# A hybrid encoder step on one core: value projection with one shared tile for the blocks' last 32 tokens, and the sampled tokens' output product with high and low parts as one operand of 64 columns

## The chip, the cores and the metric

The kernel runs on one core of a Trainium2 chip. The metric is the device time of one execution in microseconds (us), as the median of several runs. The engines are PE (matrix multiply, with PEld for the loads of its stationary operand), DVE (vector), ACT (scalar), POOL (GpSimd) and SP, which only issues transfers. Each engine works through its own queue in the order of the program that was built for it; semaphores tie the queues together. A matmul has a stationary operand of up to 128 columns and a moving operand of up to 512 columns, and adds into a bank of PSUM.

## The reference, cut to what matters

Two inputs go through the same two layers: a prompt of 2048 tokens and 32 sampled tokens that continue earlier states, 2080 tokens of width 1024 in all.

```python
# layer A: gated delta rule, then an output product and a layer norm
out = o.reshape(b, l, A_VW).astype(x.dtype) @ w_out
return layer_norm(DN_ALPHA * x + out, ln_g, ln_b), new_buf, s_new
# between the layers: one shared K and V
kv = h @ w_kv
k = rope_partial(kv[..., :B_KVW].reshape(b, l, B_KV_HEADS, B_HD), pos)
v = kv[..., B_KVW:].reshape(b, l, B_KV_HEADS, B_HD)
# layer B: sliding-window attention, then an output product and a layer norm
out = (o * jax.nn.silu(z)) @ w_out
return layer_norm(DN_ALPHA * x + out, ln_g, ln_b)
```

V has 4 heads of 64, so 256 columns. The output products are 1024 x 1024 per token.

## The kernel before, in words

All large products are in fp32 precision built from a rounded type: each operand x is split into a high part (x rounded) and a low part (x minus the high part), and a product is the sum of three matmuls, high x high, high x low and low x high. With 1024 = 8 x 128 rows to contract, a product of one tile takes 8 x 3 = 24 matmuls.

The program runs in stages. First come layer A's projections, then the delta rule over chunks of 128 tokens with the sampled tokens as a first, short chunk. Beside and behind it runs layer A's output product (class O1 with OutNorm, tile by tile of 128 tokens; the 17th and last tile holds the 32 sampled tokens). Each tile there: OutNorm.split makes the parts `ghi` and `glo` (L1091 on ACT, L1092 on DVE) while the tile before is multiplied; OutNorm.tile multiplies for two halves of 512 columns (L1105 to L1107), scales the residual and adds the product (L1110), takes statistics (L1111, L1113), forms the inverse root by Newton steps and normalizes (L1127, L1129); the rows are stored (L1186), turned by PE transposes (L1156), copied (L1158) and stored again as columns (L1160). In this stage the order on PE and DVE is that of the code.

Class P2 then reads those columns back as five blocks of 416 tokens: P2.load brings a block in four pieces over the queues of SP and ACT (L1228) into two staging buffers, and `split_acts` makes its parts (L68 on ACT, L69 on DVE for blocks 2 to 4). Blocks 0 and 1 are loaded early. P2 computes gate products (gate: L1313 to L1316, with the matmuls of `project`, L77 to L79), then the values (P2.values), then the rotated K and Q projections (P2.rotated), then more gates. From here on a scheduler sets the order on every engine by simulated times, so that instructions of a later stage may stand ahead of those of an earlier one where their buffers are free.

P2.values, at L1263 to L1276: for each block it goes through the 416 tokens in tiles of 128, 128, 128 and 32. A tile is 24 matmuls with the tokens as stationary columns and 256 value columns as the moving operand (L1272 to L1274), a copy from PSUM on ACT (L1275) and a store on SP (L1276) to the scratch `bv`. The values' weights are split at L1261 and L1262.

P2.rotated interleaves its ten slabs of weights (L46, L53, L54; five blocks each) with `keep_out_weights` (L992 to L999): layer B's output weights are read in 16 steps into one of two buffers of the pool `wo` (tag `wo_parts`), split on ACT (L995) and POOL (L996), and stored on SP (L994, L999) to the scratch `wob`, from which layer B's output stage reads them. The rotation (L1246 to L1250) uses ACT, DVE and POOL; its results are stored on SP.

Layer B's attention works on chunks of 64 queries; Attention.finish does the output product of a tile of 128 tokens: it loads the residual rows `r` (L1396, two buffers), splits (L1399 on ACT, L1400 on POOL), multiplies (L1411 to L1413), scales and adds (L1414, L1415), and normalizes either through ACT and POOL (L1424 to L1426) or, for the very last tile, on DVE (L1430, L1432), and stores `y` (L1434). The sampled tokens' tile is finished last but one, and the last tile is that of tokens 768 to 895 (the chunks run from 14 to 31 and then from 0 to 13); both take their two halves from a tile of two PSUM banks that the scores used before.

Of the kernel before, what the change touches and what calls it, by code (L numbers as in the profile page):

```python
# [10 lines left out]
F32 = mybir.dt.float32  # L11
F32R = mybir.dt.float32r
I32 = mybir.dt.int32
AF = mybir.ActivationFunctionType
ALU = mybir.AluOpType
# [4 lines left out]
D = 1024  # L20
NP = 2048
NS = 32
NT = NP + NS
TB = 416
NB = NT // TB
KC = D // 128
H = 8
ALPHA = 4.0 ** 0.25
# [67 lines left out]
class P1:  # L96
# [166 lines left out]
    def split(self):  # L263
        if self.fetched is not None:
            self.next = split_fetched(self.nc, self.wp, self.fetched, self.sub)
            self.fetched = None
# [794 lines left out]
    return gt, bt  # L1061


class OutNorm:


# [20 lines left out]
    def split(self, g, n):  # L1087
        nc = self.nc
        ghi = self.two.tile([128, KC, 128], F32R, tag="g_hi", name="g_hi")
        glo = self.two.tile([128, KC, 128], F32R, tag="g_lo", name="g_lo")  # L1090
        nc.scalar.copy(ghi[:, :, :n], g[:, :, :n])  # L1091
        nc.vector.tensor_tensor(out=glo[:, :, :n], in0=g[:, :, :n], in1=ghi[:, :, :n], op=ALU.subtract)  # L1092
        return ghi, glo

    def tile(self, parts, r, n, tail=False):

        nc, V = self.nc, self.nc.vector
        ghi, glo = parts
        st = self.two.tile([128, 2, 6], F32, tag="st", name="st")
        w = self.w  # L1100
        for c in range(2):
            cs = slice(c * 512, c * 512 + 512)
            ps = self.pp.tile([128, 512], F32, tag="po", name="po")
            for k in range(KC):
                nc.tensor.matmul(ps[:n], ghi[:, k, :n], w[0][:, k, cs], start=(k == 0), stop=False)  # L1105
                nc.tensor.matmul(ps[:n], ghi[:, k, :n], w[1][:, k, cs], start=False, stop=False)  # L1106
                nc.tensor.matmul(ps[:n], glo[:, k, :n], w[0][:, k, cs], start=False, stop=(k == KC - 1))  # L1107
                if k % 2 == 1:
                    yield 6 * 0.227
            V.scalar_tensor_tensor(out=r[:n, cs], in0=r[:n, cs], scalar=ALPHA, in1=ps[:n], op0=ALU.mult, op1=ALU.add)  # L1110
            V.bn_stats(out=st[:n, c, :], in_=r[:n, cs])  # L1111
        mv = self.two.tile([128, 2], F32, tag="mv", name="mv")
        V.bn_aggr(out=mv[:n], in_=st[:n])  # L1113
        ve = self.two.tile([128, 1], F32, tag="ve", name="ve")
        V.tensor_scalar(out=ve[:n], in0=mv[:n, 1:2], scalar1=LN_EPS, scalar2=None, op0=ALU.add)
        rs = rsqrt_newton(nc, self.two, ve, n, 1, "ln")
        tabs = self.tabs
        if not tail:
            nb = self.two.tile([128, 1], F32, tag="nb", name="nb")
            V.scalar_tensor_tensor(out=nb[:n], in0=mv[:n, 0:1], scalar=-1.0, in1=rs[:n], op0=ALU.mult, op1=ALU.mult)  # L1120
            nc.scalar.activation(r[:n], r[:n], AF.Identity, bias=nb[:n, 0:1], scale=rs[:n, 0:1])
            nc.gpsimd.tensor_tensor(out=r[:n], in0=r[:n], in1=tabs[0][:n], op=ALU.mult)
            nc.gpsimd.tensor_tensor(out=r[:n], in0=r[:n], in1=tabs[1][:n], op=ALU.add)
        else:
            for c in range(2):
                cs = slice(c * 512, c * 512 + 512)
                V.scalar_tensor_tensor(out=r[:n, cs], in0=r[:n, cs], scalar=mv[:n, 0:1], in1=tabs[0][:n, cs],  # L1127
                                       op0=ALU.subtract, op1=ALU.mult)
                V.scalar_tensor_tensor(out=r[:n, cs], in0=r[:n, cs], scalar=rs[:n, 0:1], in1=tabs[1][:n, cs],  # L1129
                                       op0=ALU.mult, op1=ALU.add)  # L1130
        yield r
# [63 lines left out]
class P2:  # L1195
# [57 lines left out]
    def values(self):  # L1253
        nc = self.nc
        vh = self.resl.tile([128, KC, 256], F32R, tag="cos", name="vh")
        vl = self.resl.tile([128, KC, 256], F32R, tag="sin", name="vl")
        for i in range(2):
            ks = slice(i * 4, i * 4 + 4)
            vr = self.wp.tile([128, 4, 256], F32, tag="w_raw", name="vr", bufs=1)
            nc.scalar.dma_start(vr[:], self.I["w_v"][:, ks, :])  # L1260
            nc.scalar.copy(vh[:, ks], vr[:])  # L1261
            nc.gpsimd.tensor_tensor(out=vl[:, ks], in0=vr[:], in1=vh[:, ks], op=ALU.subtract)  # L1262
        for b in range(NB):  # L1263
            xh, xl = self.x[b]
            for m0 in range(0, TB, 128):
                m = min(128, TB - m0)
                ms = slice(m0, m0 + m)
                a = self.wk.tile([128, 256], F32, tag="ra", name="va")
                ps = self.ps()
                po = ps[:m, 0:256]  # L1270
                for k in range(KC):
                    nc.tensor.matmul(po, xh[:, k, ms], vh[:, k, :], start=(k == 0), stop=False)  # L1272
                    nc.tensor.matmul(po, xl[:, k, ms], vh[:, k, :], start=False, stop=False)
                    nc.tensor.matmul(po, xh[:, k, ms], vl[:, k, :], start=False, stop=(k == KC - 1))  # L1274
                nc.scalar.copy(a[:m, :], po)  # L1275
                nc.sync.dma_start(self.T["bv"][b * TB + m0:b * TB + m0 + m, :], a[:m, :])  # L1276

    def rotated(self):
        nc, I, O, T = self.nc, self.I, self.O, self.T
# [39 lines left out]
class Attention:  # L1319
# [73 lines left out]
    def finish(self, t0, n, graw, late=False, tail=False):  # L1393
        nc, V, pool = self.nc, self.nc.vector, self.otwo
        r = pool.tile([128, D], F32, tag="r", name="r")
        nc.sync.dma_start(r[:n], self.T["h"][t0:t0 + n, :])  # L1396
        ghi = pool.tile([128, KC, 128], F32R, tag="g_hi", name="g_hi")
        glo = pool.tile([128, KC, 128], F32R, tag="g_lo", name="g_lo")
        nc.scalar.copy(ghi[:, :, :n], graw[:, :, :n])  # L1399
        nc.gpsimd.tensor_tensor(out=glo[:, :, :n], in0=graw[:, :, :n], in1=ghi[:, :, :n], op=ALU.subtract)  # L1400
        st = pool.tile([128, 2, 6], F32, tag="st", name="st")
        w, tabs = self.w, self.tabs
        both = self.scores_tile() if late else None
        for c in range(2):
            cs = slice(c * 512, c * 512 + 512)
            if late:
                ps = both[:, c].rearrange("p u k -> p (u k)")
            else:
                ps = self.pp.tile([128, 512], F32, tag="po", name="po")[:]
            for k in range(KC):  # L1410
                nc.tensor.matmul(ps[:n], ghi[:, k, :n], w[0][:, k, cs], start=(k == 0), stop=False)  # L1411
                nc.tensor.matmul(ps[:n], ghi[:, k, :n], w[1][:, k, cs], start=False, stop=False)  # L1412
                nc.tensor.matmul(ps[:n], glo[:, k, :n], w[0][:, k, cs], start=False, stop=(k == KC - 1))  # L1413
            V.scalar_tensor_tensor(out=r[:n, cs], in0=r[:n, cs], scalar=ALPHA, in1=ps[:n], op0=ALU.mult, op1=ALU.add)  # L1414
            V.bn_stats(out=st[:n, c, :], in_=r[:n, cs])  # L1415
        mv = pool.tile([128, 2], F32, tag="mv", name="mv")
        V.bn_aggr(out=mv[:n], in_=st[:n])
        ve = pool.tile([128, 1], F32, tag="ve", name="ve")
        V.tensor_scalar(out=ve[:n], in0=mv[:n, 1:2], scalar1=LN_EPS, scalar2=None, op0=ALU.add)
        rs = rsqrt_newton(nc, pool, ve, n, 1, "ln")  # L1420
        if not tail:
            nb = pool.tile([128, 1], F32, tag="nb", name="nb")
            V.scalar_tensor_tensor(out=nb[:n], in0=mv[:n, 0:1], scalar=-1.0, in1=rs[:n], op0=ALU.mult, op1=ALU.mult)
            nc.scalar.activation(r[:n], r[:n], AF.Identity, bias=nb[:n, 0:1], scale=rs[:n, 0:1])  # L1424
            nc.gpsimd.tensor_tensor(out=r[:n], in0=r[:n], in1=tabs[0][:n], op=ALU.mult)
            nc.gpsimd.tensor_tensor(out=r[:n], in0=r[:n], in1=tabs[1][:n], op=ALU.add)  # L1426
        else:
            for c in range(2):
                cs = slice(c * 512, c * 512 + 512)
                V.scalar_tensor_tensor(out=r[:n, cs], in0=r[:n, cs], scalar=mv[:n, 0:1], in1=tabs[0][:n, cs],  # L1430
                                       op0=ALU.subtract, op1=ALU.mult)
                V.scalar_tensor_tensor(out=r[:n, cs], in0=r[:n, cs], scalar=rs[:n, 0:1], in1=tabs[1][:n, cs],  # L1432
                                       op0=ALU.mult, op1=ALU.add)
        nc.sync.dma_start(self.O["y"][t0:t0 + n, :], r[:n])  # L1434
# [374 lines left out]
```

## Time and profile before

| what | us |
|---|---|
| median of three runs | 2256.95 |
| lowest and highest of them | 2256.91, 2264.41 |
| the profiled execution | 2253.47 |
| its span in the trace | 2251.5 |

The profile is of one execution. Its page gives busy times of each engine as a share of the span, the chain of work that ended last (followed back from the end through whatever released each step), and groups of instructions by line. In a row of a group, "x16 | 6.4, 396 | 0.8" means 16 instructions, 6.4 us busy, 396 ns each by the trace, and 0.8 us in which the engine sat idle just before them. A matmul's recorded duration holds its way through the array, so that neighbours overlap: the pace of matmuls is read from the distance between their starts. In the rows of the timeline, the first number is the start in us from the start of the span, the second the duration, and square brackets give an idle time before it with what ended it. In stretches of the span, each engine's busy time stands with its number of instructions, followed by the granted clock of PE as a share of full speed, the share of time in which the transfer engines were busy, and their rate.

### The profile page before, as it was taken

How to read it: one execution, taken by the hardware profiler on the slowest of the kernel's cores; microseconds unless marked ns; L12 is line 12 of the kernel's file. 1: busy time of each engine (PE TensorE's matmuls, PEld its weight loads, DVE VectorE, ACT ScalarE, POOL GpSimd, SP SyncE). 2: the span in 40 equal slices, each digit the busy share in tenths (PEclk: the TensorE clock that was granted, in tenths of full speed). 3: DMA queues.
4: the chain of work that ended last, by engine and by line, in shares of the span. 5: the costliest groups of instructions: out<-in, count | busy, mean ns of one | idle time of the engine just before them, and what ended most of it. 6: DMA issues, size and time to landing. Idle time of an engine off the chain costs nothing.

```text
span 2251.5 us, 36813 instructions
## 1 busy us (share of the span) xinstructions
PE 2180.5 (97%) x13810; PEld 1996.7 (89%) x13810; DVE 1372.5 (61%) x2709; ACT 897.3 (40%) x2230; POOL 836.6 (37%) x1185
## 2 busy tenths in 40 slices
PE   8999999999999999999899999999999999999997
PEld 6999999999999888898888887999999987778884
DVE  3666566743486677778868874124442235668774
ACT  4444444433223666667641212311112235445541
POOL 1422121212111577767721201324442124556563
PEclk9999999999999999999999999999999999999999
DMA  5222222323534243335526765732122277233311
GB/s 193 67 70 74 72 71 69 109 92 117 143 106 152 95 136 121 121 127 202 188 96 209 227 189 166 244 131 75 66 73 73 83 177 251 75 94 96 111 61 52
DMA packets 250530, 274.49 MB, mean 122 GB/s; under 512 B 76096, under 2 KB 195200, under 8 KB 250080
## 3 DMA queue, kind: packets, MB, share of 16 engines
q1 hardware_dynamic: 238352, 248.84, 35.2%
q10 hardware_dynamic: 12000, 23.30, 2.9%
q8 instruction: 109, 1.79, 0.3%
q14 instruction: 69, 0.57, 0.1%
HBM read 168.53 MB, written 103.92 MB: 121 GB/s over the span
## 4 chain that ended last, share of the span: by engine, by line
PE 84%; ACT 7%; DVE 4%; DMA 2%; POOL 2%; issue 1%; ACTq 0%; SPq 0%; DVEq 0%; POOLq 0%
PE ps L77 16%; PE ps L79 16%; PE ps L78 16%; PE ot L1526 4%; PE po L1105 3%; PE po L1107 3%; PE po L1106 3%; PE po L1411 2%; PE po L1413 2%; PE po L1412 2%; PE S L1505 2%; PE tr L1520 2%; PE vp L714 1%; ACT kd L588 1%; PE op L732 1%
## 5 line engine op out<-in xcount | busy, mean ns | idle before, releaser
L77 PE MATMUL ps<-act_hi,w_hi 128*128 128x416 f32 x2000 | 707.0, 354 | 8.2 <-ACT act_hi L68 4.5
L79 PE MATMUL ps<-act_hi,w_lo 128*128 128x416 f32 x2000 | 705.1, 353 | 1.8 <-POOL w_lo L54 1.2
L78 PE MATMUL ps<-act_lo,w_hi 128*128 128x416 f32 x2000 | 701.9, 351 | 0.1
L77 PEld LDWEIGHTS ps<-act_hi,w_hi 128*128 128x128 f32 x2000 | 377.0, 189 | 13.6 <-ACT act_hi L68 5.2
L79 PEld LDWEIGHTS ps<-act_hi,w_lo 128*128 128x128 f32 x2000 | 376.1, 188 | 6.7 <-POOL w_lo L54 1.7
L78 PEld LDWEIGHTS ps<-act_lo,w_hi 128*128 128x128 f32 x2000 | 376.4, 188 | 5.1 <-DVE act_lo L69 0.8
L54 POOL TENSOR_TENSOR w_lo<-w_raw,w_hi 128x1024 fp32r<-128x1024 f32 x51 | 135.3, 2652 | 547.9 <-ACT w_hi L53 490.8
L196 DVE SCALAR_TENSOR_TENSOR y<-R,convw,y 128x2083 f32<-128x2083 f32 x72 | 173.7, 2414 | 109.7 <-ACT y L194 74.2
L572 POOL TENSOR_TENSOR tm<-L,Tt 128x60 f32<-128x60 f32 (+19 forms) x373 | 139.7, 375 | 123.7 <-DVE tm L572 51.7
L1513 POOL TENSOR_TENSOR P<-P,sm 128x384 f32<-128x384 f32 (+2 forms) x128 | 100.5, 807 | 180.0 <-DVE sm L1390 102.4
L575 POOL TENSOR_TENSOR Tt<-Tt,tm 128x60 f32<-128x60 f32 (+19 forms) x373 | 152.9, 410 | 29.2
L1386 ACT ACTIVATE P<-S,nm 128x192 f32<-128x192 f32 (+2 forms) x260 | 104.6, 418 | 93.7 <-DVE nm L1379 40.7
L227 ACT COPY R<-ps 128x416 f32<-128x416 f32 (+1 forms) x144 | 61.2, 448 | 199.2 <-PE ps L79 174.4
L53 ACT CAST w_hi<-w_raw 128x1024 fp32r<-128x1024 f32 x62 | 65.0, 1048 | 137.4 <-PE ps L78 111.8
L1248 POOL TENSOR_TENSOR rs<-rs,sin 128x416 f32<-128x416 f32 x50 | 71.2, 1424 | 116.3 <-DVE rs L1247 102.0
L1105 PE MATMUL po<-wo_hi,g_hi 128*128 128x512 f32 (+1 forms) x272 | 110.2, 405 | 1.8 <-DVE r L1110 1.1
L1107 PE MATMUL po<-wo_hi,g_lo 128*128 128x512 f32 (+1 forms) x272 | 106.9, 393 | 0.0
L1106 PE MATMUL po<-wo_lo,g_hi 128*128 128x512 f32 (+1 forms) x272 | 106.6, 392 | 0.0
L1526 PE MATMUL ot<-pt,vd 128*128 128x256 f32 x372 | 98.7, 392 | 1.6 <-ACT pt L1522 1.2
L1411 PE MATMUL po<-wo,g_hi 128*128 128x512 f32 x240 | 99.4, 414 | 0.0
L1413 PE MATMUL po<-wo,g_lo 128*128 128x512 f32 x240 | 96.2, 401 | 0.0
L1412 PE MATMUL po<-wo,g_hi 128*128 128x512 f32 x240 | 96.1, 400 | 0.0
(284 smaller groups left out, 4002.0 us busy)
## 6 DMA issues: line engine op xcount, KB each, us to landing
w_raw<-in_w_in SPq DMA_DIRECT2D x40, 512.0 KB
w_raw<-in_b_w_in SPq DMA_DIRECT2D x20, 512.0 KB
gb<-s_gcum SPq DMA_DIRECT2D x17, 512.0 KB
k<-s_k SPq DMA_DIRECT2D x17, 512.0 KB
s_bz<-za SPq DMA_DIRECT2D x40, 208.0 KB
s_bq<-ra SPq DMA_DIRECT2D x40, 208.0 KB
s_q<-y SPq DMA_DIRECT2D x8, 1024.0 KB
s_k<-y SPq DMA_DIRECT2D x8, 1024.0 KB
```

The costliest lines, as they stand in the source:

```text
L77: nc.tensor.matmul(ps, hi[:, k, :], xh[:, k, :], start=(k == 0), stop=False)
L78: nc.tensor.matmul(ps, hi[:, k, :], xl[:, k, :], start=False, stop=False)
L79: nc.tensor.matmul(ps, lo[:, k, :], xh[:, k, :], start=False, stop=(k == KC - 1))
L196: nc.vector.scalar_tensor_tensor(out=y[:], in0=R[:, j:j + W], scalar=self.convw[:, i, j:j + 1], in1=y[:], op0=ALU.mult, op1=ALU.add)
L575: P.tensor_tensor(out=Tt[:n, i0:, :w], in0=Tt[:n, i0:, :w], in1=tm[:n, i0 - k:, :w], op=ALU.subtract)
L1105: nc.tensor.matmul(ps[:n], ghi[:, k, :n], w[0][:, k, cs], start=(k == 0), stop=False)
L1106: nc.tensor.matmul(ps[:n], ghi[:, k, :n], w[1][:, k, cs], start=False, stop=False)
L1107: nc.tensor.matmul(ps[:n], glo[:, k, :n], w[0][:, k, cs], start=False, stop=(k == KC - 1))
L1411: nc.tensor.matmul(ps[:n], ghi[:, k, :n], w[0][:, k, cs], start=(k == 0), stop=False)
L1412: nc.tensor.matmul(ps[:n], ghi[:, k, :n], w[1][:, k, cs], start=False, stop=False)
L1413: nc.tensor.matmul(ps[:n], glo[:, k, :n], w[0][:, k, cs], start=False, stop=(k == KC - 1))
L1526: nc.tensor.matmul(ot[:, p], self.vd[:, kc0 + j, p, :], pt[:, 2 * j:2 * j + 2, :], start=(j == 0), stop=(j == nj - 1))
```

## The change

In P2.values the last 32 tokens of blocks 0 to 3 are gathered in one tile of 128: for each of them the high part is copied by ACT and the low part by POOL into two operands (`eh`, `el`) that lie in the two buffers of the pool `wo`. The five blocks' 15 full tiles are computed first, then the shared tile, stored in four pieces of 32 rows, then the last 32 tokens of block 4 (the sampled tokens) as a tile of their own.

In the output products of both layers, a tile of at most 64 tokens (only the sampled one) has its low part written beside the high part in `ghi`, columns 32 to 63. A matmul with those 64 stationary columns against the high weights gives high x high in 32 rows of PSUM and low x high in the next 32; a second matmul adds high x low weights to the first 32 rows. The two halves are added behind the scaling: ACT copies the second half from PSUM into the room of `glo`, and DVE adds it.

```diff
+def low_part(ghi, glo, n):
+    return ghi[:, :, n:2 * n] if n <= 64 else glo[:, :, :n]
+
+def out_products(nc, ps, ghi, glo, w, k, cs, n):
+    a, z = k == 0, k == KC - 1
+    if n <= 64:
+        nc.tensor.matmul(ps[:2 * n], ghi[:, k, :2 * n], w[0][:, k, cs], start=a, stop=z, skip_group_check=True)
+        nc.tensor.matmul(ps[:n], ghi[:, k, :n], w[1][:, k, cs], start=False, stop=z, skip_group_check=True)
+        return
+    nc.tensor.matmul(ps[:n], ghi[:, k, :n], w[0][:, k, cs], start=a, stop=False)
+    nc.tensor.matmul(ps[:n], ghi[:, k, :n], w[1][:, k, cs], start=False, stop=False)
+    nc.tensor.matmul(ps[:n], glo[:, k, :n], w[0][:, k, cs], start=False, stop=z)
+
+def add_products(nc, r, glo, ps, cs, n):
+    V = nc.vector
+    V.scalar_tensor_tensor(out=r[:n, cs], in0=r[:n, cs], scalar=ALPHA, in1=ps[:n], op0=ALU.mult, op1=ALU.add)
+    if n <= 64:
+        second = glo[:].bitcast(F32).rearrange("p k t -> p (k t)")[:n, cs]
+        nc.scalar.copy(second, ps[n:2 * n])
+        V.tensor_tensor(out=r[:n, cs], in0=r[:n, cs], in1=second, op=ALU.add)
...
@@ OutNorm.split
-        nc.vector.tensor_tensor(out=glo[:, :, :n], in0=g[:, :, :n], in1=ghi[:, :, :n], op=ALU.subtract)
+        nc.vector.tensor_tensor(out=low_part(ghi, glo, n), in0=g[:, :, :n], in1=ghi[:, :, :n], op=ALU.subtract)
@@ OutNorm.tile (and the same in Attention.finish, without the yield)
-                nc.tensor.matmul(ps[:n], ghi[:, k, :n], w[0][:, k, cs], start=(k == 0), stop=False)
-                nc.tensor.matmul(ps[:n], ghi[:, k, :n], w[1][:, k, cs], start=False, stop=False)
-                nc.tensor.matmul(ps[:n], glo[:, k, :n], w[0][:, k, cs], start=False, stop=(k == KC - 1))
+                out_products(nc, ps, ghi, glo, w, k, cs, n)
                 if k % 2 == 1:
-                    yield 6 * 0.227
-            V.scalar_tensor_tensor(out=r[:n, cs], in0=r[:n, cs], scalar=ALPHA, in1=ps[:n], op0=ALU.mult, op1=ALU.add)
+                    yield (4 if n <= 64 else 6) * 0.227
+            add_products(nc, r, glo, ps, cs, n)
@@ P2.values
+        full = TB // 128 * 128
+        rows = TB - full
+        eh, el = (self.wo.tile([128, 2, D // 2], F32R, tag="wo_parts", name="x_rest")[:].rearrange(
+            "p a (b t) -> p (a b) t", t=128) for _ in range(2))
+        for b in range(NB - 1):
+            xh, xl = self.x[b]
+            rs = slice(b * rows, b * rows + rows)
+            nc.scalar.copy(eh[:, :, rs], xh[:, :, full:TB])
+            nc.gpsimd.tensor_copy(el[:, :, rs], xl[:, :, full:TB])
         for b in range(NB):
             xh, xl = self.x[b]
-            for m0 in range(0, TB, 128):
...
+            for m0 in range(0, full, 128):
+                a = self.value_tile(xh[:, :, m0:m0 + 128], xl[:, :, m0:m0 + 128], vh, vl)
+                nc.sync.dma_start(self.T["bv"][b * TB + m0:b * TB + m0 + 128, :], a[:])
+        a = self.value_tile(eh, el, vh, vl)
+        for b in range(NB - 1):
+            nc.sync.dma_start(self.T["bv"][b * TB + full:b * TB + TB, :], a[b * rows:b * rows + rows, :])
+        xh, xl = self.x[NB - 1]
+        a = self.value_tile(xh[:, :, full:TB], xl[:, :, full:TB], vh, vl)
+        nc.sync.dma_start(self.T["bv"][NT - rows:NT, :], a[:rows, :])
...
@@ Attention.finish
-        nc.gpsimd.tensor_tensor(out=glo[:, :, :n], in0=graw[:, :, :n], in1=ghi[:, :, :n], op=ALU.subtract)
+        nc.gpsimd.tensor_tensor(out=low_part(ghi, glo, n), in0=graw[:, :, :n], in1=ghi[:, :, :n], op=ALU.subtract)
```

The new function `value_tile` holds the 24 matmuls and the copy that stood in the loop.

More of the change, by code (lines that the diff above doesn't have):

```diff
@@ L1263, in values @@
         for b in range(NB):
             xh, xl = self.x[b]
-            for m0 in range(0, TB, 128):
[L1266 to L1276, printed above, removed]
+            for m0 in range(0, full, 128):
+                a = self.value_tile(xh[:, :, m0:m0 + 128], xl[:, :, m0:m0 + 128], vh, vl)
+                nc.sync.dma_start(self.T["bv"][b * TB + m0:b * TB + m0 + 128, :], a[:])
@@ new lines, in values, with value_tile @@
+        a = self.value_tile(eh, el, vh, vl)
[4 more added lines that the diff above has]
+        nc.sync.dma_start(self.T["bv"][NT - rows:NT, :], a[:rows, :])
+    def value_tile(self, xh, xl, vh, vl):
+        nc, m = self.nc, xh.shape[2]
+        a = self.wk.tile([128, 256], F32, tag="ra", name="va")
+        po = self.ps()[:m, 0:256]
+        for k in range(KC):
+            nc.tensor.matmul(po, xh[:, k, :], vh[:, k, :], start=(k == 0), stop=False)
+            nc.tensor.matmul(po, xl[:, k, :], vh[:, k, :], start=False, stop=False)
+            nc.tensor.matmul(po, xh[:, k, :], vl[:, k, :], start=False, stop=(k == KC - 1))
+        nc.scalar.copy(a[:m, :], po)
+        return a
@@ L1410, in finish @@
             for k in range(KC):
[L1411 to L1414, printed above, removed]
+                out_products(nc, ps, ghi, glo, w, k, cs, n)
+            add_products(nc, r, glo, ps, cs, n)
             V.bn_stats(out=st[:n, c, :], in_=r[:n, cs])
```

## The prediction

> **What bounds the kernel now.** I read the page's busy times first, then its chain of work that ended last, then the busy times in stretches around the lines that change.
>
> ```profile
> span 2251.5 us, 36813 instructions
> PE 2180.5 (97%) x13810; PEld 1996.7 (89%) x13810; DVE 1372.5 (61%) x2709; ACT 897.3 (40%) x2230; POOL 836.6 (37%) x1185
> PE 84%; ACT 7%; DVE 4%; DMA 2%; POOL 2%; issue 1%; ACTq 0%; SPq 0%; DVEq 0%; POOLq 0%
> ```
>
> PE is busy 97% of the span and holds 84% of the chain. A matmul that goes away is worth its pace, wherever PE does not wait for something else. Where it waits is shown by the stretches (columns: stretch, length, busy time of PE, PEld, DVE, ACT, POOL, then granted clock, DMA share, GB/s):
>
> ```profile
> 1338.00:1374.00 36.00, 36.00 (x177) 26.95 (x176) 23.00 (x54) 3.10 (x6) 0.00 (x0) 1.00 0.32 102
> 1396.00:1417.00 21.00, 16.36 (x90) 15.21 (x89) 7.31 (x9) 9.82 (x17) 5.44 (x4) 0.92 0.88 300
> 1417.00:1440.00 23.00, 23.00 (x170) 22.68 (x169) 6.38 (x5) 10.02 (x18) 9.64 (x7) 1.00 0.78 260
> 1440.00:1478.00 38.00, 38.00 (x326) 37.19 (x325) 0.00 (x0) 8.15 (x22) 11.14 (x8) 1.00 0.58 202
> 1478.00:1640.00 162.00, 162.00 (x860) 160.66 (x858) 69.56 (x139) 25.08 (x43) 64.06 (x41) 1.00 0.23 81
> ```
>
> Layer A's sampled tile (in the first stretch), most of the value projection (third and fourth) and the rotated projections behind it (fifth) run on a PE without a gap. Two places are different: 1396 to 1417, where PE lacks 4.6 of 21 us and its clock is 0.92, and the tail (below).
>
> **Value projection: fewer tiles.** Before there are 15 tiles of 128 tokens and 5 of 32, each of 24 matmuls. After, 15 of 128, one of 4 x 32 = 128, and one of 32. Starts of a small tile, of the full tile behind it, and of the next:
>
> ```profile
> 1452.81 0.11 PEld L1272 LDWEIGHTS ps<-vh,act_hi 128*32 128x32 f32 x1
> 1455.60 0.19 PEld L1272 LDWEIGHTS ps<-vh,act_hi 128*128 128x128 f32 x1
> 1458.44 0.19 PEld L1272 LDWEIGHTS ps<-vh,act_hi 128*128 128x128 f32 x1
> ```
>
> A small tile takes 2.79 us, a full one 2.84: the 256 moving columns set the pace, not the tokens. Four small tiles go and one full comes: -4 x 2.79 + 2.84 = **-8.3 us**. What is added is building the shared tile: 4 copies of 128x256 on ACT and 4 on POOL. The nearest rows are a cast and a subtraction of that size:
>
> ```profile
> L1399 ACT CAST g_hi<-graw 128x256 fp32r<-128x256 f32 x1 | 0.4, 404 | 7.0 <-DVE graw L1475 7.0
> 2215.04 0.74 POOL L1400 TENSOR_TENSOR g_lo<-graw,g_hi 128x256 fp32r<-128x256 f32 x1 [6.28 <-ACT g_hi L1399]
> ```
>
> That is 4 x 0.40 = 1.6 us on ACT and 4 x 0.74 = 3.0 us on POOL. I cost them at 0: the shared tile is computed behind 15 full tiles (43 us), and the stretch from 1440 has ACT busy 8.15 and POOL 11.14 of 38 us. Without that cover PE would wait the longer of the two, 3.0 us. SP still issues five stores of 32 rows, four of them later than now.
>
> **The sampled tokens' product, twice.** Of 24 matmuls for each half of the columns, 16 remain: high and low part lie side by side as 64 stationary columns against the high weights, and the high part alone meets the low weights. 16 fewer in layer A and 16 in layer B. Pace in layer A, first and eleventh of such a row, and the cost by stationary columns in layer B:
>
> ```profile
> 1360.60 0.40 PE L1105 MATMUL po<-wo_hi,g_hi 128*32 128x512 f32 x1
> 1362.91 0.39 PE L1106 MATMUL po<-wo_lo,g_hi 128*32 128x512 f32 x1
> L1411 PE MATMUL S<-wo,g_hi 128*128 128x512 f32 x16 | 6.4, 401 | 1.1 <-DVE r L1414 1.1
> L1411 PE MATMUL S<-wo,g_hi 128*32 128x512 f32 x16 | 6.3, 396 | 0.8 <-ACT g_hi L1399 0.8
> ```
>
> (1362.91 - 1360.60) / 10 = 0.231 us each. 32 columns and 128 cost the same (396 and 401 ns), so 64 lie between. Each place saves 16 x 0.231 = 3.7 us of PE.
>
> In layer A the low part is split one tile ahead, so the first matmul does not wait longer. The halves must now be added: a copy on ACT beside the scaling on DVE, then an add on DVE. For the first half 3.7 us of the second half's matmuls hide that. For the second it lies on the chain to the stored rows and the casts behind them:
>
> ```profile
> 1371.00 0.59 ACT L1158 COPY hT<-ps 128x512 f32<-128x512 f32 x1 [9.28 <-issue]
> L1110 DVE SCALAR_TENSOR_TENSOR r<-r,po 32x512 f32<-32x512 f32 x2 | 1.3, 672 | 2.1 <-PE po L1107 2.1
> L1250 DVE TENSOR_TENSOR ra<-ra,rs 128x416 f32<-128x416 f32 x50 | 29.6, 592 | 48.0 <-POOL rs L1248 47.9
> 1380.09 0.32 SPq L1186 DMA_DIRECT2D s_h<-r  x1
> 1382.82 1.70 ACT L68 CAST act_hi<-act_raw 128x832 fp32r<-128x832 f32 x2
> ```
>
> The copy (0.59) ends within the scaling (0.67), the add is about 0.6 x 512/416 = 0.7. The chain gains 3.7 - 0.7 = 3.0, PE itself 3.7. The casts feed the stretch in which PE waits, so I take **-3.0**.
>
> **Layer B, in the tail.** Pieces of the chain, in order, then the same matmul and the last vector steps in the timeline:
>
> ```profile
> 2228.97 3.56 DMA r<-s_h
> 2232.68 0.68 DVE r L1414
> 2241.21 2.42 issue
> ...
> 2215.02 0.42 PE L1411 MATMUL S<-wo,g_hi 128*32 128x512 f32 x1 [0.82 <-ACT g_hi L1399]
> 2233.40 0.50 PE L1411 MATMUL S<-wo,g_hi 128*128 128x512 f32 x1 [1.13 <-DVE r L1414]
> 2240.82 2.33 POOL L1426 TENSOR_TENSOR r<-r,ln_b 32x1024 f32<-32x1024 f32 x1
> 2241.07 3.29 DVE L1430 SCALAR_TENSOR_TENSOR r<-r,mv,ln_g 128x512 f32<-128x512 f32 x2
> ```
>
> The last 24 matmuls start at 2233.40 because the last tile's residual rows arrive at 2232.5, by a buffer that an earlier tile's output frees; PE already waits 1.13 us. The shorter product ahead of them only makes that wait longer. It also starts later: the low part now lies in the first operand, so the first matmul waits for POOL's subtraction (quoted above: 2215.04 + 0.74) instead of running at 2215.02. That is 0.8 us, and all of PE's queue stands behind it. New wait: 1.13 + 3.7 - 0.8 = 4.0 us. The gain, if any, is on DVE: its two steps of 0.75 take 3.29 while POOL finishes the sampled rows, a stall of 2.42. If the sampled tile ends 2 to 3 us sooner, POOL is done before them. If the queue on DVE puts the sampled tile's new add behind the last tile's scaling, it ends 0.7 later instead. Bounds -2.4 and +0.7; I take **-1.0**, as the stall is the nearest row and its end depends on an order not shown.
>
> **What the shared tile displaces.** Its two operands take the two buffers through which layer B's output weights are split and stored (16 steps). In the trace those steps start early:
>
> ```profile
> L992 SPq DMA_DIRECT2D wo_parts<-in_b_w_out x16: 328/346/602, 1383.4 to 1466.6; - x16
> L996 POOL TENSOR_TENSOR wo_parts<-wo_parts x16: 1286/1294/2024, 1388.0 to 1470.4; 128x512 fp32r<-128x512 f32 x16
> 1383.40 3.26 DMA wo_parts<-in_b_w_out
> 1386.69 4.84 DMA act_raw<-s_hT
> 1394.30 7.06 DMA s_wob<-wo_parts
> 1401.81 5.83 DMA act_raw<-s_hT
> PE ps L77 <- ACT act_hi L68: 4.5, 2, 3.2
> ```
>
> On SP and ACT they stand ahead of the loads of blocks 2 to 4, and the chain runs through them from 1383 to 1407; PE waits 4.5 us for those casts. After the change no step can begin before the shared tile's last matmul, so the loads have the queues and the DMA to themselves. All 16 steps move into the rotated projections, where DMA share is 0.23 and POOL is busy 64 of 162 us; 16 x 1.29 more fits. Nothing reads the stored parts before layer B's output stage. Bounds: -5.4 (4.5 of waiting and 0.9 of slow clock behind it, below) and 0 if the casts are late for their own DMA time; a loss is a rival below. I take the middle, **-3.0**.
>
> **Slow clock, and a rule against the change.** After the 3.16 us wait the same 256-column matmul has another pace:
>
> ```profile
> 1400.20 1.06 PE L77 MATMUL ps<-act_hi,w_hi 128*128 128x416 f32 x2 [3.16 <-ACT act_hi L68]
> 1401.06 0.42 PE L1272 MATMUL ps<-vh,act_hi 128*128 128x256 f32 x1
> 1402.98 0.36 PE L1272 MATMUL ps<-vh,act_hi 128*128 128x256 f32 x1
> ```
>
> Nine take 1.92 us, 0.213 each against 2.84 / 24 = 0.118, which costs 0.9 us. After the 1.13 us wait at 2233.40 there is no such row. The tail's new wait of 4.0 us is longer than 3.16, so its last 24 matmuls may start at that pace: 2.8 us (1400.20 to 1402.98) of slow running at 0.118 / 0.213 of the pace loses 1.2 us. The Trainium skill, page "TensorE: Matmul & The Clock Gate", section "Why this matters for your kernels", warns of PE gaps over about 3 us, which bring half the clock. By that rule the tail loses the 1.2; by a rule of work removed alone it does not.
>
> **Sum.** -8.3 - 3.0 - 1.0 - 3.0 = -15.3 us. The profiled execution took 2253.47 (2.0 more than its span), 3.5 under the median of the runs, 2256.95. The stretches behind the change are assumed to move as a whole. Forecast 2256.95 - 15.3 = **2241.6 us**.
>
> **Rivals.**
> 1. *Full gain:* the waits before 1417 vanish (-5.4), layer A gives 3.7, the tail 2.4: -8.3 - 3.7 - 2.4 - 5.4 = -19.8, 2237.2. For it: all these waits lead to the displaced steps or to the sampled tile. Against: loads take 4.8 to 5.8 us each, some of it their own.
> 2. *Cold tail:* -8.3 - 3.0 + 1.2 - 3.0 = -13.1, 2243.8.
> 3. *The displacement is worth nothing*, and the tail neither: -11.3, 2245.7. For it: the order of the queues is laid out anew, and another load may be late.
> 4. *Slower:* the 16 steps, now among the rotated projections, stand on SP ahead of a slab's weight load. The steps took 1383 to 1472, 5.6 us each. One such round in front of each of five slabs without cover is 28 us; -11.3 + 28 = +17, 2274. It decides from 2.3 us a slab. Against: a slab's weights are fetched while the one before it is multiplied, 120 matmuls of 162 / 860 = 0.188 us or 22.6 us, four rounds of steps.
> 5. *It doesn't do what it says:* 64 columns cost more than 32. The rows at 32 and 128 exclude it; 1%.
>
> **How the numbers follow.** Forecast (2239 to 2244.5) 0.40; full gain 0.15; cold tail 0.16; nothing from the displacement 0.20, a quarter of it below 2245.7; given back in the rotated stage, in part or with a loss, 0.08, of which 0.05 beyond 2268; the fifth 0.01. About 0.5%, 11.3 us, is what a measurement of this kernel can tell from no change. Faster: 0.40 + 0.15 + 0.16 + 0.05 = 0.76, less 0.04 for the spread of runs, 0.72; slower 0.05; same the rest, 0.23. The range takes in all but the slower cases and the far end of the full gain: 2235 to 2250.
>
> **What would show it.** Value matmuls 408 in place of 480 at 0.117 us; no step of the output weights before the shared tile, and a PE wait well under 4.5 us at blocks 2 to 4; sampled products 16 a half in both layers; in the tail a PE wait near 4 us ahead of the last 24 matmuls, their first ones slow or not, and DVE's last scaling without the 2.4 us stall. The forecast is wrong if PE shows gaps among the rotated projections, or if the waits before 1417 stay.

## The result, and the profile after

The changed kernel took 2234.68 us (median of 4 runs, 2233.65 to 2245.97) against 2258.88 of the kernel before (4 runs, 2256.91 to 2264.41), a ratio of 0.991 with a 95% interval of 0.9887 to 0.9933. Two later comparisons with more runs gave 2238.60 against 2255.67 (0.9923, 0.9903 to 0.9943) and 2239.07 against 2256.35 (0.992, 0.9894 to 0.9946). By these ratios, which are not those of the medians, it is faster by 17 to 20 us (by the medians 24, 17 and 17). The forecast, 2241.6 of 2256.95, is a ratio of 0.9932, inside all three intervals, in the slower half of each. The profiled execution took 2235.55 us, 17.9 below the one of before.

The page of the changed kernel: its span, busy times and chain.

```profile
span 2233.8 us, 36601 instructions
PE 2161.8 (97%) x13706; PEld 1982.5 (89%) x13706; DVE 1378.5 (62%) x2713; ACT 900.5 (40%) x2235; POOL 838.1 (38%) x1189
PE 83%; ACT 7%; DVE 4%; DMA 3%; POOL 1%; issue 1%; ACTq 0%; DVEq 0%; SPq 0%; POOLq 0%
```

PE lost 18.7 us of busy time and keeps its 97%. The two value-projection stretches that answer to 1396–1417 and 1478–1640 of before, counted from the next gate's first matmul and from the last value matmul:

```profile
1390.62:1411.62 21.00, 20.21 (x120) 19.22 (x119) 9.15 (x11) 9.16 (x16) 0.51 (x2) 1.00 0.63 187
1459.60:1621.60 162.00, 162.00 (x860) 160.66 (x858) 75.56 (x139) 33.82 (x59) 84.06 (x57) 1.00 0.46 157
```

In the first, PE lacks 0.8 us in place of 4.6, its clock is 1.00 in place of 0.92, and the DMA share fell from 0.88 to 0.63. The second is the rotated projections: they received the 16 weight steps (POOL 64.06 to 84.06, DMA 0.23 to 0.46), and PE still has no gap. The rows of these steps, of the value matmuls, of the wait for the casts and of the sampled product in layer A:

```profile
L992 SPq DMA_DIRECT2D wo_parts<-in_b_w_out x16: 327/346/532, 1457.3 to 1530.5; - x16
L1315 PE MATMUL ps<-vh,act_hi 128*128 128x256 f32 (+1 forms) x128 | 35.9, 281 | 0.0
L1315 PE MATMUL ps<-vh,x_rest x8: 277/280/282, 1454.3 to 1456.8; 128*128 128x256 f32 x8
PE ps L77 <- ACT act_hi L68: 0.6, 2, 0.4
L1073 PE MATMUL po<-wo_hi,g_hi 128*64 128x512 f32 x16 | 6.3, 396 | 0.0
```

Each of the three value lines has 128 + 8 matmuls, 408 in all. 64 stationary columns cost what 32 do (396 ns).

To see where the time went I cut each trace at the same five places. These rows are the cuts of before (the first cut, 1360.60, stands in the prediction), then of after: the sampled product's first matmul, the next gate's first matmul, the last value matmul, and the sampled tile's rounded copy in the tail.

```profile
1372.51 0.43 PE L77 MATMUL ps<-act_hi,w_hi 128*128 128x416 f32 x1
1478.21 0.28 PE L1274 MATMUL ps<-vl,act_hi 128*32 128x256 f32 x1
2214.56 1.35 ACT L1399 CAST g_hi<-graw 128x256 fp32r<-128x256 f32 x2 [7.04 <-DVE graw L1475]
```

```profile
1358.95 0.39 PE L1073 MATMUL po<-wo_hi,g_hi 128*64 128x512 f32 x1
1367.13 0.44 PE L77 MATMUL ps<-act_hi,w_hi 128*128 128x416 f32 x1
1459.83 0.28 PE L1317 MATMUL ps<-vl,act_hi 128*32 128x256 f32 x1
2198.23 1.35 ACT L1442 CAST g_hi<-graw 128x256 fp32r<-128x256 f32 x2 [7.04 <-DVE graw L1516]
```

| us | before | after | difference |
|---|---|---|---|
| start to the sampled product of layer A | 1360.60 | 1358.95 | -1.65 |
| its product, to the next gate | 11.91 | 8.18 | -3.73 |
| to the last value matmul | 105.70 | 92.70 | -13.00 |
| to the sampled tile's rounded copy | 736.35 | 738.40 | +2.05 |
| tail, to the end | 36.94 | 35.57 | -1.37 |
| span | 2251.5 | 2233.8 | -17.7 |

The first line is no effect of the change, since all that runs ahead of it is the same. The experiments show which of the others are.

### The profile page after: what moved, and what is told of

Read it like the earlier page. It is cut to its first block, busy times and chain, and to the rows that moved or that the text cites. A ratio compares the mean times of both kernels' runs of the same rounds, so it can differ in the third digit from the quotient of the medians.

```text
span 2233.8 us, 36601 instructions
## 1 busy us (share of the span) xinstructions
PE 2161.8 (97%) x13706; PEld 1982.5 (89%) x13706; DVE 1378.5 (62%) x2713; ACT 900.5 (40%) x2235; POOL 838.1 (38%) x1189
## 4 chain that ended last, share of the span: by engine, by line
PE 83%; ACT 7%; DVE 4%; DMA 3%; POOL 1%; issue 1%; ACTq 0%; DVEq 0%; SPq 0%; POOLq 0%
PE ps L77 16%; PE ps L79 16%; PE ps L78 16%; PE po L1076 5%; PE po L1078 4%; PE po L1077 4%; PE ot L1567 4%; PE S L1546 2%; PE tr L1561 2%; PE vp L714 1%; DMA act_raw<-s_hT 1%; ACT kd L588 1%; PE op L732 1%; PE sp L744 1%; PE gq L618 1%
## 5 line engine op out<-in xcount | busy, mean ns | idle before, releaser
L77 PEld LDWEIGHTS ps<-act_hi,w_hi 128*128 128x128 f32 x2000 | 376.8, 189 | 11.9 <-ACT w_hi L53 6.1
L1076 PE MATMUL po<-wo_hi,g_hi 128*128 128x512 f32 x256 | 103.8, 406 | 1.8 <-ACT hT L1183 1.8
L1078 PE MATMUL po<-wo_hi,g_lo 128*128 128x512 f32 x256 | 100.6, 393 | 0.0
L1077 PE MATMUL po<-wo_lo,g_hi 128*128 128x512 f32 x256 | 100.3, 392 | 0.0
```

The source lines that it names most:

```text
L77: nc.tensor.matmul(ps, hi[:, k, :], xh[:, k, :], start=(k == 0), stop=False)
```

## Experiments

**My theory:** value work -8.3; the steps' later place -4.4 to -4.8; layer A -3.7; in the tail the last tile's residual load decides, so that the narrower product brings little there. **Rival:** the place of the steps is worth nothing, and what the value stage gained beyond 8.3 comes with the gathered tile. Each profile was cut as above:

| kernel | product, layer A | to last value matmul | tail |
|---|---|---|---|
| before | 11.91 | 105.70 | 36.94 |
| after, three executions | 8.18 | 92.70, 92.75, 91.63 | 35.57, 37.88, 37.10 |
| own buffers | 8.18 | 97.07 | 37.13 |
| hold only | 11.91 | 100.91 | 38.55 |
| values only | 11.92 | 91.87 | 36.95 |
| products only | 8.18 | 106.94 | 37.12 |
| layer A only | 8.17 | 91.48 | 36.96 |
| third residual | 8.18 | 92.61 | 32.67 |
| second bank | 8.17 | 93.48 | 31.47 |
| both of these | 8.17 | 92.84 | 31.55 |

From the last value matmul to layer B's first scores it is 341.83 us in every one of them.

### The place of the 16 steps: own buffers, hold only

Own buffers: the change, with the steps free to start early.

```diff
+        self.xr = new_pool(self.tc, left, "p2_xr", 2, side="left")
...
-        eh, el = (self.wo.tile([128, 2, D // 2], F32R, tag="wo_parts", name="x_rest")[:].rearrange(
+        eh, el = (self.xr.tile([128, 2, D // 2], F32R, tag="x_rest", name="x_rest")[:].rearrange(
```

> The changed kernel, but the gathered 32-token pieces have a pool of their own, so the 16 output-weight steps need not wait for the value matmuls and stand early on the queues again; the matmul work is that of the changed kernel. Theory (the steps' place is worth about 4.7 us, by keeping the value matmuls fed with activations): 12 to 13.5 us below before instead of 17.7, PE's wait ps <- act_hi before about 1417 back at 4 to 5 us, and the last value matmul 8 to 9 us earlier than before's, not 13. Rival (the place is worth nothing, and the 4.7 us came from the gathered tile itself): 17 to 18 us below before, and the wait for act_hi stays under 1 us.

Measured 2243.12 against 2255.24, ratio 0.9937 (0.9923 to 0.995), which is 14.2 us (11.3 to 17.4) and does not by itself exclude the rival's 17. The trace decides. The steps are early again, PE's wait is back, and the stretch looks like that of before, but for the clock:

```profile
L992 SPq DMA_DIRECT2D wo_parts<-in_b_w_out x16: 333/346/710, 1384.4 to 1466.1; - x16
PE ps L77 <- ACT act_hi L68: 4.0, 3, 2.4
1396.08:1417.08 21.00, 16.62 (x97) 15.13 (x96) 8.66 (x9) 11.40 (x19) 6.13 (x5) 1.00 0.92 318
```

The last value matmul comes 97.07 us after the cut, 8.6 sooner than in before and 4.4 later than in the first execution of the changed kernel, whose matmuls are the same. The rival asked for no difference.

Hold only: before, with the steps held and nothing saved. Copies of the last 32 tokens of four blocks go into the two buffers, and only the last small tile is computed from them.

```diff
+        eh, el = (self.wo.tile([128, 2, D // 2], F32R, tag="wo_parts", name="x_rest")[:].rearrange(
+            "p a (b t) -> p (a b) t", t=128) for _ in range(2))
+        for b in range(1, NB):
...
+                if b == NB - 1 and m < 128:
+                    xh, xl, ms = eh, el, slice(b * 32 - 32, b * 32)
```

(My expectation below says 25 value tiles; there are 20.)

> The kernel before, with only the hold put in: block pieces are copied into the two weight buffers, and only the last small value tile is computed from them, so the 16 steps are held until then, while all 25 value tiles are still computed as in before. Theory (the place of the steps is worth 4.7 us): 4 to 5.5 us below before, the wait ps <- act_hi under 1 us. Rival (the steps' place is worth nothing): within 1 us of before. Second rival (the held steps cost as much in the rotated projections as they save): within 1 us, with the loss to be seen as PE idle between the last value matmul and the first attention scores.

Measured 2250.94 (12 runs) against 2255.24, ratio 0.9983 (0.9968 to 0.9999).

```profile
L992 SPq DMA_DIRECT2D wo_parts<-in_b_w_out x16: 328/334/451, 1482.3 to 1554.8; - x16
PE ps L77 <- ACT act_hi L68: 0.2, 1, 0.2
1403.95:1424.95 21.00, 20.53 (x118) 19.25 (x116) 9.52 (x12) 9.91 (x17) 0.70 (x2) 1.00 0.64 190
```

With 20 tiles as in before, the stage is 4.8 us shorter, and the wait is gone. The second rival falls too: the rotated stage takes the same 341.83. Both runs agree on 4.4 to 4.8 us, each from one profile a side: the eight executions with the changed value stage and held steps range from 91.48 to 93.48, so such a size is good to about 1 us.

In the profiled execution of hold only the tail took 38.55 us, though its product is the old one: a stretch of half clock fell on it (last section).

Whether the early steps hurt by their transfers or by their places on SP and ACT no experiment separates, but the traces speak for the places. In before, between 1383 and 1420, SP stood 11.9 us at the steps' reads and stores, with loads of blocks behind them in its queue; in the changed kernel no such wait stands in the stretch. The load that went out at 1401.81 on the chain of before stood directly behind a step's read. The loads themselves are no slower there: 4.84 and 5.83 us on that chain, and in the changed kernel's 3.84 to 6.17. Before, then two loads of the changed kernel:

```profile
SPq L992 <- DMA s_wob<-wo_parts: 6.9, 4, 2.7
SPq L994 <- POOL wo_parts L996: 5.0, 3, 3.4
1401.38 0.33 SPq L992
```

```profile
1385.21 4.86 DMA act_raw<-s_hT
1392.07 6.17 DMA act_raw<-s_hT
```

### The two halves of the change alone: values only, products only

Values only sets the threshold of 64 tokens in the three product functions to 0; products only puts the loop of before back into `values`.

```diff
-    if n <= 64:
+    if n <= 0:
```

> The changed kernel's value projection, with the sampled tokens' output products as three operands of 32 columns as in before. Theory: the value tiles' work 8.3 us plus the steps' place 4.7 us, 13 us below before (12 to 14); the next gate's first matmul as long after layer A's sampled products as in before (11.9 us). Rival (value work alone counts): 8 to 9 us below.

> The changed kernel's sampled output products, with the value projection of before. Theory: layer A's product 3.7 us and the tail 1.4 us, 4.5 to 5.5 us below before; the steps stand early, and the wait ps <- act_hi is 4 to 5 us as in before. In the tail, a POOL wait of about 1.6 us ahead of the sampled product with some 7 matmuls at half pace behind it. Rival (the tail gives nothing, because its end is set by the last full tile's residual load): 3.5 to 4 us below.

Values only: 2245.33 against 2255.24, ratio 0.9946 (0.9932 to 0.9959), which is 12.2 us by the ratio (9.2 to 15.3) and 9.9 by the medians. Its value stage is 13.8 us shorter and layer A's product as in before, as the theory has it. In the profiled execution 4.5 us went astray in the first 25 us of layer B's output products: in the first ten PE waits 2.67 us for ACT (0.69 in before), and the clock behind is low (values only, then the same stretch of before):

```profile
1868.10:1878.10 10.00, 7.33 (x25) 5.45 (x24) 5.59 (x16) 5.14 (x21) 6.73 (x8) 0.66 1.07 371
```

```profile
1880.17:1890.17 10.00, 9.12 (x51) 6.98 (x50) 6.44 (x16) 7.35 (x31) 8.92 (x8) 1.00 1.07 377
```

Products only: 2253.05 against 2255.24, ratio 0.9989 (0.9975 to 1.0003). By the whole time that is 2.5 us (-0.7 to 5.6), not to be told from nothing. 3.73 us went in layer A, the tail is 0.2 longer than in before, and the value stage, where PE waits for the casts as in before, took 106.94 us in place of 105.70, so that 2.5 us are left at the last value matmul. That is the miss of its expectation: I took 1.4 us for the tail from the one profile of the changed kernel, and theory and rival (3.5 to 4, which is nearer) both counted layer A's saving in full.

### The tail: the change again, layer A only, third residual, second bank

> The changed kernel once more. From the four runs before: value work 8.3 us, steps' place 4.4 to 4.8, layer A's product 3.7, sum 16.5 us below before, give or take the stretches of half clock. Theory of the tail (the last tile's residual load ends it, whatever the sampled product takes): 37 us from the sampled tile's rounded copy to the end, with a wait of 2 to 4 us ahead of the last 24 matmuls. Rival (the tail is 1.4 us shorter for good, as in the one profile of the changed kernel): 35.5 us.

Measured 2238.60 against 2255.67. The tail took 37.88 us, and its critical wait is the one that was forecast, with the first matmuls behind it slow (0.63 us each, 0.43 apart from the second on):

```profile
2216.77 0.79 PE L1076 MATMUL S<-wo,g_hi 128*128 128x512 f32 x1 [3.59 <-DVE r L1084]
2217.37 0.63 PE L1077 MATMUL S<-wo,g_hi 128*128 128x512 f32 x1
```

Layer A only: the tail's sampled product is written as before, in `finish`.

```diff
-                out_products(nc, ps, ghi, glo, w, k, cs, n)
-            add_products(nc, r, glo, ps, cs, n)
+                nc.tensor.matmul(ps[:n], ghi[:, k, :n], w[0][:, k, cs], start=(k == 0), stop=False)
+                nc.tensor.matmul(ps[:n], ghi[:, k, :n], w[1][:, k, cs], start=False, stop=False)
+                nc.tensor.matmul(ps[:n], glo[:, k, :n], w[0][:, k, cs], start=False, stop=(k == KC - 1))
```

> The changed kernel, with the sampled product of layer B (in the tail) as three operands of 32 columns as in before; layer A's keeps the 64 columns. Theory (the tail's saving of 3.7 us of matmul time is swallowed by the wait for the residual load): within 1 us of the changed kernel, the wait ahead of the last 24 matmuls back at 1.1 us, 36.9 us from the rounded copy to the end. Rival (the narrower product in the tail gives 1.4 us): 1 to 2 us slower than the changed kernel.

Measured 2240.17 (7 runs, 2232.05 to 2251.16), ratio 0.9931 (0.9903 to 0.9959): not to be told from the changed kernel's 2238.60. The medians' difference, 1.57, would suit the rival too; the tail does not: it is 36.96 us, that of before, with a wait of 1.14, and no longer than the changed kernel's in the middle (37.1).

Third residual gives the residual rows a third buffer, which lifts the last tile's load ahead of the store it stood behind:

```diff
-        r = pool.tile([128, D], F32, tag="r", name="r")
+        r = pool.tile([128, D], F32, tag="r", name="r", bufs=3)
```

> The changed kernel with a third buffer for the residual rows of the output tiles, so that the last tile's load goes out ahead of the store that it stood behind. Theory: the wait ahead of the last 24 matmuls falls to 1.0 to 1.3 us, and the end comes 2.3 us sooner after the rounded copy (34.8 us instead of 37.1). Rival (POOL's work or PE's own pace ends the tail): no change of the end, and the wait stays.

Second bank: in the last two tiles the second half of the columns uses another bank, so it need not wait for the drain of the first half.

```diff
-            if late:
+            if late and c == 0:
```

> The changed kernel, with the second half of the output columns of the last two tiles summed in the bank of the tiles before, so that these matmuls need not wait for the drain of the first half. Theory: no wait ahead of the last 24 matmuls; PE ends 3 to 3.7 us sooner, and the end 3 us sooner (34 us after the rounded copy), the residual load now covered by these matmuls. Rival (the drain that waits for the load then ends the tail just as late): under 1 us sooner.

Third residual: 2240.45, ratio 0.9927 (0.9906 to 0.9948). Second bank: 2236.54, ratio 0.9917 (0.9895 to 0.9938). By the whole time neither can be told from the changed kernel, but the tails are 32.67 and 31.47 us, shorter than expected (34.8 and 34). The last tile's load in the changed kernel, 15.0 us behind the rounded copy; then, in third residual, the load, 3.0 us ahead of the copy, and the last 24 matmuls' start:

```profile
2213.22 0.32 SPq L1439 DMA_DIRECT2D r<-s_h  x1
```

```profile
2200.67 0.32 SPq L1439 DMA_DIRECT2D r<-s_h  x1
2220.07 0.50 PE L1076 MATMUL S<-wo,g_hi 128*128 128x512 f32 x1 [0.84 <-DVE ln_y L434]
```

The drains in second bank:

```profile
2221.22 0.69 DVE L1084 SCALAR_TENSOR_TENSOR r<-r,S 128x512 f32<-128x512 f32 x1 [2.52 <-DMA r<-s_h]
2223.69 0.69 DVE L1084 SCALAR_TENSOR_TENSOR r<-r,po 128x512 f32<-128x512 f32 x1 [1.05 <-PE po L1078]
```

In second bank DVE still waits for the load, but PE is then at work on the second half; the last drain waits for PE. The expectations left out that a short wait also spares the slow matmuls behind it: the starts of the last 24 span 5.47 us in third residual, 7.01 in own buffers behind a wait of 3.69. Both edits together:

> The changed kernel with both of the last two edits: the second halves in the bank of the tiles before, and the third buffer for the residual rows. Theory (both take away the same wait; with the bank alone, the load lands while PE is still at work, so PE's own pace ends the tail): 31 to 32 us from the sampled tile's rounded copy to the end, as with the bank alone, no wait ahead of the last 24 matmuls; 4 to 6 us below the changed kernel of the same call. Rival (two separate gains that add): 27 us.

> The changed kernel beside the one above, on the same chip, to compare the two. All theories: 16 to 18 us below before, 35.5 to 38 us from the rounded copy to the end; 4 to 6 us above the kernel with both edits.

Measured 2236.97 with both (ratio 0.9917, 0.989 to 0.9944) and 2239.07 for the change beside it. The tail is 31.55, as with the bank alone: they take away the same wait. This version beats the change by 5.5 us in the tail (37.10 against 31.55); in the whole time the difference of medians is 2.1, and the intervals overlap, so that a gain over the change is shown for the tail only, and the 4 to 6 us expected of the whole time are not. Against before it is faster.

## Why the prediction was right, and where not

- **Value tiles, -8.3:** right. Between own buffers and before, with the steps in the same place, the stage lost 8.6 us; other pairs with the steps in one place give 9.0 (hold only and values only) and 9.9 (products only and own buffers). The copies that build the shared tile were free: PE waits for none of them.
- **Displacement, -3.0:** the mechanism was right, the size too small: 4.4 to 4.8, near the far end (-5.4) of the bounds. I took the middle because the casts might be late by their own transfers; they are not, the wait falls to 0.2–0.6 us. The slow clock behind the wait, which before had in this stretch (0.92), goes with it; own buffers had the wait at a clock of 1.00, so not every execution pays these 0.9 us of the bound. The slower rival, steps ahead of weight loads, did not occur: 341.83 us in every profile.
- **Layer A, -3.0:** mis-sized. The nine profiles with the new product show 8.17 or 8.18 us, the three others 11.91 or 11.92: PE's own 16 x 0.231 = 3.7. The term took off 0.7 for the added vector step because the casts feed a stretch that waits; with the steps held that wait is gone. This reason is argued, not tested alone. It fits that products only, where the wait stays, kept 2.5 of its 3.73 us at the last value matmul, near the -3.0.
- **Layer B's tail, -1.0:** this step failed as a size: the tail brought nothing. The rows show its three pieces. First, the load starts the last 24 matmuls 19.3 us after the rounded copy in place of 18.84. Second, DVE's stall did go, as the lower bound had it; the two steps that took 3.29 us in before:

```profile
2225.18 1.40 DVE L1471 SCALAR_TENSOR_TENSOR r<-r,mv,ln_g 128x512 f32<-128x512 f32 x2
2217.51 0.50 PE L1076 MATMUL S<-wo,g_hi 128*128 128x512 f32 x1 [2.28 <-DVE r L1084]
```

  Third, a wait of 3.59 to 3.69 us (forecast 4.0) is followed by slow matmuls in four of the five executions that have the new product and the old bank and buffers: from the last 24 matmuls' start to the end they take 17.8 to 18.6 us, in place of 16.3 in the one above, where the wait was 2.28. There the sampled product itself ran at half clock, so that PE came later to the wait. So in most executions the tail is the *cold tail* of the second rival, offset by the stall: 0.4 for the later start and 1.5 for the slow matmuls, less 1.9 of stall, leave 37.1 in the middle against 36.94, no gain. The prediction had seen the stall and the slow matmuls, but counted the slow matmuls in a rival only.
- **The +2.05 between the value matmuls and the tail** was not foreseen, and is not the change's. PE's wait there for a weight cast on ACT varies (2.2 us in before, 4.1 in the changed kernel's first execution), and with it the time: the stretch from layer B's first scores to its first output product took 57.6 to 62.2 us in the eight profiles with the changed value stage and held steps (60.1 on average), and 59.3 to 60.2 in the four others (59.8).
- **The sum:** -8.6 - 4.4 - 3.7 and nothing in the tail make -16.7, against -15.3 forecast. The two sizes that were too small outweigh the tail that was too large, so that the sum is nearer than its terms: that part is luck. The first comparison's 20 us is also the *full gain* of the first rival (-19.8), but two of that rival's terms did not come: the tail's 2.4 not at all, and of the displacement's 5.4 not all. The bare median 2234.68 lies 0.3 below the stated range of 2235 to 2250; by the ratios, on 2256.95, the three comparisons give 2236.6, 2239.6 and 2238.9.

## What to carry to other kernels

Where a small tile costs as much as a full one, what counts is the number of passes over the moving operand: gather small tiles, or set two operands side by side in the stationary columns. Look at what the gathering's buffers hold up: here, work held back into a stage with idle engines and transfers gave about half as much as the saving itself, on top of it. Matmuls saved ahead of a load that sets the end, as in this tail, only lengthen the wait for it; take that wait away first, by a buffer or a bank.

## What the runs showed of the hardware

**Half clock comes in whole stretches of 3.41 us, and not only after long gaps.** In each of the twelve traces every change of the granted clock lies on one grid of 3.41 us, and half clock lasts one, two or three of its stretches, until the matmuls end. Two executions of the same changed kernel, cut on their own grids. The first:

```profile
2195.75:2199.16 3.41, 2.11 (x11) 0.95 (x10) 1.87 (x5) 0.93 (x2) 0.45 (x1) 1.00 0.15 38
2199.16:2202.57 3.41, 3.08 (x8) 1.45 (x9) 1.97 (x13) 1.36 (x2) 0.28 (x1) 0.50 0.00 0
```

The one beside the last experiment:

```profile
2196.07:2199.49 3.42, 2.32 (x10) 1.27 (x11) 2.66 (x15) 1.37 (x3) 0.73 (x1) 1.00 0.00 0
2199.49:2202.90 3.41, 2.44 (x11) 1.23 (x10) 1.08 (x2) 1.63 (x2) 2.27 (x1) 1.00 0.00 0
```

Both have the same longest wait, 1.63 us for POOL's subtraction, and only the first is granted 0.50 behind it; the grid lies otherwise to the wait. In hold only, a wait of 0.82 was enough, and cost its tail some 1.6 us:

```profile
2215.60:2219.01 3.41, 2.44 (x12) 0.89 (x10) 2.13 (x7) 1.26 (x2) 0.74 (x1) 1.00 0.13 38
2219.01:2222.43 3.42, 3.40 (x8) 1.37 (x9) 3.18 (x8) 0.10 (x1) 2.41 (x1) 0.50 0.00 0
```

Neither PE's busy time in the stretch ahead nor that of the weight loads decides it alone. In third residual, 1.63 and 0.97 us kept the full clock:

```profile
2224.30:2227.71 3.41, 1.63 (x8) 0.97 (x6) 1.64 (x4) 0.00 (x0) 3.18 (x2) 1.00 0.00 0
2227.71:2231.13 3.42, 0.00 (x0) 0.00 (x0) 3.07 (x14) 0.00 (x0) 0.00 (x0) 1.00 0.17 38
```

In the change beside the last experiment, 1.37 and 1.15 us lost it:

```profile
2213.14:2216.55 3.41, 1.37 (x6) 1.15 (x7) 1.38 (x2) 0.20 (x1) 3.05 (x2) 1.00 0.19 77
2216.55:2219.97 3.42, 3.42 (x10) 2.64 (x9) 0.00 (x0) 0.00 (x0) 1.65 (x1) 0.50 0.17 38
```

That the stretches lie on a grid of their own is what the Trainium skill says, page "TensorE: Matmul & The Clock Gate", section "Part 1: The HAM clock gate (the "warmup" mystery)": an activity window of about 3.4 us that runs free of the kernel. The durations here agree. The advice of the Trainium skill, same page, section "Why this matters for your kernels", against PE gaps over some 3 us does not cover these cases: gaps of 1.63 and 0.82 us with small products around them were enough. Which activity counts was not tested by an experiment and stays open.

**This makes executions of one program differ ahead of any change.** Layer A's sampled product began at 1358.27 to 1368.55 us in the twelve profiles, though the instructions up to there are the same. The half clock granted from 15 us on up to that point adds up to 23.9 us in the earliest execution (both edits) and to 58.0 in the latest (hold only). Hold only and before, in one stretch of layer A:

```profile
1060.00:1100.00 40.00, 37.71 (x352) 35.23 (x350) 31.66 (x79) 28.53 (x90) 26.68 (x71) 0.87 0.51 176
```

```profile
1060.00:1100.00 40.00, 35.07 (x386) 32.36 (x387) 35.24 (x87) 29.06 (x92) 29.87 (x82) 0.99 0.59 211
```

At a clock of 0.87 it got through 352 matmuls, at 0.99 through 386. Effects of 1 to 5 us are therefore better read between two cuts of the same trace than from whole times.
